# Macaron trunk on one core: four direct pairs of feed-forward tiles instead of six, the quads' input forms made product by product, and a ring of four weight units in the hybrid mixer

## The chip, the cores and the metric

The kernel runs on one core of a Trainium2 chip. The metric is the device time of one execution, in microseconds. Before the change it was run three times: the median is 1932.62 us, the lowest 1932.16, the highest 1934.15.

## What is computed

Two layers over 512 tokens of width 1024, in float32. Each layer is a feed-forward, a token mixer and a second feed-forward; the mixer of layer 0 is the hybrid one (retention and dilated attention side by side), that of layer 1 is stick-breaking attention. So there are four feed-forwards, each of hidden width 2816:

```python
def swiglu_ffn(x, g, w_in, w_out):
    h = rms_norm(x, g)
    gate, up = jnp.split(h @ w_in, 2, axis=-1)
    return (jax.nn.silu(gate) * up) @ w_out

for layer in range(DEPTH):
    x = x + 0.5 * swiglu_ffn(x, ffn1_norm[layer], ...)
    x = x + (retention_dilated_mixer if layer % 2 == 0 else stick_breaking_mixer)(x, ...)
    x = x + 0.5 * swiglu_ffn(x, ffn2_norm[layer], ...)
return rms_norm(x, final_norm)
```

## The kernel before, in words

**Three products for one.** Activations lie transposed, 128 features by 512 tokens a tile. Each float32 operand is split into a high and a low part of type float32r, and a product is made of three matmuls: high by high, high by low, low by high (`mm3`). A weight tile is 128x1024 (512 KB). It is loaded by SyncE's DMA queue into a raw slot (role `wraw`), and its parts stand in two slots of role `whl`. Two ways lead there. `weight` has ScalarE cast the high part (L224) and VectorE subtract it from the raw tile (L225). `weight_dma`, used for the hybrid mixer's input projections, has ScalarE cast the high part (L195), then make minus the high part in the slot of the low one (L196), and then a DMA from GpSimd's queue adds the weight again from DRAM (L197), so that VectorE has no part in it.

**A feed-forward** (`ffn_seven`) has 22 hidden tiles, each with a gate and an up tile. The first `DIRECT` = 6 pairs are projected directly: 24 matmuls of 512 columns for gate, as many for up. Before the first pair comes the norm's mean over the features (TensorE, role `po`), from which ScalarE and VectorE make `rr`. The other 16 hidden tiles are made by 8 quads (`quad`). A quad takes the four quarter tiles of two hidden tiles (a11, a12, a21, a22) and makes seven products (`product`: 24 matmuls of 256 columns each) in the manner of Winograd's form of Strassen's method: T3, T1, T4, B11, T2, B22, B21 by the name of the form of the input that each takes. The forms are sums and differences of quarters of the normed input, made once per feed-forward from `x` and `rr` by `normed_forms`, all before the first quad (L431 to L440, then split into high and low parts at L224 and L225). The sums of a quad's own weights are made by VectorE (p3 at L479, p1 at L485, p2 at L491, p4 at L495) and split (`cut_form`); the weights that need no sum go through ScalarE and GpSimd's queue (`cut_raw`, L450 to L452), but in the first quad of a feed-forward (`early`) a22 and a11 are split by VectorE.

**The output of a feed-forward** (`out_ffn`) has 8 tiles of 66 matmuls, whose weights come in three pieces by `weight`. Beside it runs work ahead of time for the mixers, two or so units a tile: `cut_ahead` splits a weight of the stick-breaking mixer and stores both parts to DRAM, `centre` takes the mean off a value weight of the retention heads and stores it. There are 40 such units: 16 beside the first output, 12 beside the second and 12 beside the third.

**The hybrid mixer** projects four gate tiles (`hyb_g`), then q and k of head pair 0 (`hyb_rq`, `hyb_rk`), then values of a group of heads (`values`: two weight tiles, 16 steps of six matmuls of 256 columns), and so on. A stream of projection steps is interleaved with attention: `flow.run(26)`, then the scores of head 0 (`begin(0)`), then `flow.run(27)`. After a q or k projection VectorE rotates the tile, ScalarE and VectorE split it, and `pack_q` or `pack_k` moves its halves by SyncE's queue (L654) into the layout that the scores take. 

**What sets the order.** All big tiles share 43 slots of SBUF, which roles use in turn: four slots `wraw` and six `whl` (three weight units) in the direct pairs, outputs and mixers; seven and ten in the quads. An instruction that writes a slot waits until all that read it before are done. TensorE's order is that of the program wherever `order["on"]` is set; on the other engines a scheduler puts instructions in order by their place in the program, moved ahead by `high_priority(offset)`. Every engine and every issuing queue works through its list strictly in order.

## Time and profile before

| | us |
|---|---|
| median of three runs | 1932.62 |
| the profiled execution | 1934.09 |
| span of its trace | 1932.4 |
| first feed-forward: direct pairs, quads, output | 8 to 74, 74 to 236, 236 to 357 |
| hybrid mixer | 357 to 621 |
| second feed-forward | 621 to 970 |
| third feed-forward | 970 to 1317 |
| stick-breaking mixer | 1317 to 1572 |
| fourth feed-forward and final norm | 1572 to 1932 |

The borders are read from the chain of work that ended last, rounded to whole microseconds. The trace is of one execution. "PE" is TensorE's matmuls, "PEld" its weight loads, "DVE" VectorE, "ACT" ScalarE, "POOL" GpSimd, "SPq" SyncE's sequencer issuing DMAs. Tiles are named by role. Nearly every matmul is recorded at one line (L126), so a stage is found by tiles and time, not by line. The execution's time is 1.7 us more than the span, which is what lies around it.

### The profile page before, as it was taken

The page shows a single profiled execution, that of the slowest core. Times are in us where ns is not written, and L with a number is a line of the kernel's source. Part 1 is how long each engine was busy: PE and PEld are TensorE (multiplying, and loading weights), DVE is VectorE, ACT ScalarE, POOL GpSimd, SP SyncE. Part 2 cuts the span into 40 slices and gives each one's busy share as a digit, 9 for nine tenths or more (in the row PEclk, how much of TensorE's full clock was granted, in tenths as well). Part 3 has the DMA queues.
Part 4 walks back from the last instruction along what each step waited for, and adds up shares of the span by engine and source line. Part 5 has one row for each costly group of instructions (what it writes and reads, how often), then busy time and mean ns, then how long its engine had stood idle before and what let it go on. Part 6 is the DMA issues. An engine that isn't in the chain of part 4 may idle for free.

```text
span 1932.4 us, 29858 instructions
## 1 busy us (share of the span) xinstructions
PE 1910.3 (99%) x11648; PEld 1716.8 (89%) x11648; DVE 1304.9 (68%) x1854; ACT 1059.0 (55%) x1506; POOL 165.8 (9%) x285
## 2 busy tenths in 40 slices
PE   9999999989999999999999999999999999999998
PEld 7999988778888899998889999888888888999887
DVE  8767855346777877674477677443888878777534
ACT  6466734545776456663344567332666644666423
POOL 0011000112100001100000110000222200111000
PEclk9999999999999999999999999999999999999999
DMA  6386689889852457767734775667555443767433
GB/s 228 101 202 167 140 277 338 249 225 237 178 131 84 140 140 180 167 192 254 276 131 110 197 170 148 208 225 232 161 185 152 137 137 104 201 164 163 117 92 121
DMA packets 107837, 341.00 MB, mean 176 GB/s; under 512 B 13232, under 2 KB 14896, under 8 KB 107696
## 3 DMA queue, kind: packets, MB, share of 16 engines
q1 hardware_dynamic: 90992, 278.54, 44.0%
q0 software_dynamic: 16560, 60.30, 18.0%
q8 instruction: 91, 1.49, 0.3%
q14 instruction: 50, 0.41, 0.1%
q10 hardware_dynamic: 144, 0.26, 0.0%
HBM read 280.33 MB, written 37.75 MB: 165 GB/s over the span
## 4 chain that ended last, share of the span: by engine, by line
PE 94%; DMA 3%; DVE 2%; issue 1%; ACT 1%; SPq 0%; POOL 0%; DVEq 0%; ACTq 0%; POOLq 0%
PE acc L126 46%; PE att L126 45%; PE po L126 2%; DVE whl L225 1%; DMA whl<-centred 1%; PE att L129 0%; DMA cut_sb_k<-whl 0%; DMA qk<-ah 0%; DMA qk<-sp 0%; DVE h L256 0%; DMA cut_sb_v<-whl 0%; DMA wraw<-f_out 0%; ACT whl L224 0%; DMA x<-xT 0%; DMA cut_sb_q<-whl 0%
## 5 line engine op out<-in xcount | busy, mean ns | idle before, releaser
L224 ACT CAST whl<-wraw 128x1024 fp32r<-128x1024 f32 (+4 forms) x308 | 302.8, 989 | 459.0 <-PE acc L126 199.9
L225 DVE TENSOR_TENSOR whl<-wraw,whl 128x1024 fp32r<-128x1024 f32 (+4 forms) x308 | 352.2, 1147 | 259.2 <-ACT whl L224 232.2
L126 PE MATMUL acc<-u,whl 128*128 128x512 f32 (+1 forms) x2244 | 483.5, 377 | 2.1 <-DVE whl L225 2.1
L126 PEld LDWEIGHTS acc<-u,whl 128*128 128x128 f32 x2244 | 403.3, 188 | 80.8 <-DVE whl L225 3.7
L126 PE MATMUL att<-fT,whl 128*128 128x256 f32 x3072 | 379.1, 283 | 0.0
L126 PEld LDWEIGHTS att<-fT,whl 128*128 128x128 f32 x3072 | 373.5, 192 | 0.3
L126 PE MATMUL acc<-h,whl 128*128 128x512 f32 x1248 | 302.1, 394 | 0.9 <-DVE whl L225 0.6
L126 PE MATMUL att<-fB,whl 128*128 128x256 f32 x2304 | 287.2, 283 | 0.0
L126 PEld LDWEIGHTS att<-fB,whl 128*128 128x128 f32 x2304 | 281.2, 192 | 0.2 <-DMA whl<-wq 0.2
L126 PEld LDWEIGHTS acc<-h,whl 128*128 128x128 f32 x1248 | 232.8, 188 | 53.1 <-issue 2.9
L452 POOL DMA_DIRECT2D whl<-wq x88 | 76.4, 868 | 1022.4 <-ACT whl L451 763.0
L450 ACT CAST whl<-wraw 128x1024 fp32r<-128x1024 f32 x88 | 92.4, 1050 | 83.8 <-PE att L126 83.8
L126 PE MATMUL att<-h,whl 128*128 128x512 f32 x576 | 135.8, 389 | 0.0
L126 PEld LDWEIGHTS att<-h,whl 128*128 128x128 f32 x576 | 108.4, 188 | 22.6
L451 ACT ACTIVATE whl<-whl 128x1024 fp32r<-128x1024 f32 x88 | 93.3, 1060 | 2.7
L225 DVE TENSOR_TENSOR whl<-p,whl 128x1024 fp32r<-128x1024 f32 x32 | 39.2, 1224 | 69.5 <-ACT whl L224 69.5
L126 PE MATMUL acc<-whl,h 128*128 128x256 f32 x576 | 75.9, 287 | 4.3 <-DMA whl<-centred 4.3
L126 PEld LDWEIGHTS acc<-whl,h 128*128 128x128 f32 x576 | 73.4, 194 | 5.8 <-DMA whl<-centred 4.7
L323 DVE SCALAR_TENSOR_TENSOR x<-acc,x 128x512 f32<-128x512 f32 (+1 forms) x34 | 22.4, 658 | 69.5 <-PE acc L126 69.4
L225 DVE TENSOR_TENSOR u<-uq,u 128x512 fp32r<-128x512 f32 x88 | 58.9, 688 | 13.4 <-ACT u L224 12.8
L936 POOL TENSOR_SCALAR_AFFINE_SELECT t<-t 128x128 f32<-128x128 f32 x128 | 46.2, 383 | 190.0 <-DVE t L953 124.4
L224 ACT CAST u<-uq 128x512 fp32r<-128x512 f32 x88 | 52.6, 617 | 17.3 <-PE att L126 10.3
(184 smaller groups left out, 2171.8 us busy)
## 6 DMA issues: line engine op xcount, KB each, us to landing
wraw<-wq SPq DMA_DIRECT2D x128, 512.0 KB, 5.0
whl<-wq POOLq DMA_DIRECT2D x88, 512.0 KB, 6.9
wraw<-f_out SPq DMA_DIRECT2D x68, 448.0 KB, 4.3
wraw<-wd SPq DMA_DIRECT2D x46, 512.0 KB, 3.7
wraw<-f_out SPq DMA_DIRECT2D x34, 512.0 KB, 4.7
cut_sb_q<-whl SPq DMA_DIRECT2D x16, 512.0 KB, 3.8
cut_sb_k<-whl SPq DMA_DIRECT2D x16, 512.0 KB, 3.5
cut_sb_v<-whl SPq DMA_DIRECT2D x16, 512.0 KB, 4.8
```

The costliest lines, as they stand in the source:

```text
L126: return ordered(nc.tensor.matmul(*args, **kw))
L224: nc.scalar.copy(out=hi, in_=src)
L225: nc.vector.tensor_tensor(out=lo, in0=src, in1=f32(hi), op=ALU.subtract)
L323: nc.vector.scalar_tensor_tensor(out=x[d][:, sl], in0=ps[:, sl], scalar=0.5, in1=x[d][:, sl], op0=ALU.mult, op1=ALU.add)
L450: nc.scalar.copy(out=hi, in_=raw)
L451: nc.scalar.mul(out=lo, in_=f32(hi), mul=-1.0)
L452: nc.gpsimd.dma_start(lo, src, accum_op=ALU.add)
L936: nc.gpsimd.affine_select(out=t[:, at:at + P], in_=t[:, at:at + P], pattern=[[1, P]], compare_op=ALU.is_gt, fill=0.0, base=0, channel_mult ...
```

## The change

1. `DIRECT` is 4: each feed-forward projects four pairs directly and makes nine quads instead of eight. Of the four pairs, the weights of the last two go through `weight_dma`.
2. `normed_forms` becomes a generator. It makes the eight normed tiles at once, but each form (difference and split) only as the product that takes it comes up in the program. The first quad has a22 cut by `cut_raw` ahead of its first product; a11 alone is still split by VectorE there.
3. `weight_dma` makes minus the high part straight from the raw tile (`minus_hi`) and lets the DMA go; the high part comes after it in the program.
4. In the hybrid mixer two of the four raw slots become `whl` slots: eight of them, four weight units. The scores of head 0 come after 32 steps of the stream instead of 26 (21 instead of 27 follow), and the gates are finished after three gate projections instead of two.
5. Work ahead of time: 12, 14 and 14 units beside the three outputs, and the four `centre` units come fifth to eighth instead of first.
6. Priorities: the first weight pieces of an output tile 0 and the sums of the norm are moved ahead; in the later feed-forwards the norm's mean stands one step (three matmuls) ahead of the end of the first up projection.
7. The slots of the quads' rings are the same in number (seven, ten and one), taken from other tiles.

```diff
-DIRECT = 6
+DIRECT = 4
...
+    def minus_hi(lo, src, raw):
+
+        nc.scalar.mul(out=lo, in_=raw, mul=-1.0)
+        nc.gpsimd.dma_start(lo, src, accum_op=ALU.add)
+
     def weight_dma(src, cols):
...
         nc.sync.dma_start(raw[:, :cols], src)
+        minus_hi(lo, src, raw[:, :cols])
         nc.scalar.copy(out=hi, in_=raw[:, :cols])
-        nc.scalar.mul(out=lo, in_=f32(hi), mul=-1.0)
-        nc.gpsimd.dma_start(lo, src, accum_op=ALU.add)
         return hi, lo
...
-        while pending:
-            norm_sum(*pending.pop(0))
+        with tc.high_priority(offset=2 * FIRST):
+            while pending:
+                norm_sum(*pending.pop(0))
...
-            w = weight(src[:, p0 * P:(p0 + m) * P], m * P)
+            with tc.high_priority(offset=soon):
+                w = weight(src[:, p0 * P:(p0 + m) * P], m * P)
...
-    def normed_forms(rr, gcol, work):
+    def normed_forms(rr, gcol, work, sums):
+
+        give(tf=work, tt=sums)
+        hn = []
...
+        def form(n, src):
+            fm[n] = []
+            for t in src:
+                o = B((P, 2, 2, HT), F32R, "f" + n)
+                split(o[:, 0], o[:, 1], t)
+                fm[n].append(o)
+
+        def less(a, b, sign=1.0):
+
+            t = B((P, 2, 2, HT), F32, "tt")
+            for kk in range(2):
+                nc.vector.scalar_tensor_tensor(out=t[:, kk], in0=a[kk], scalar=sign, in1=b[kk],
+                                               op0=ALU.mult, op1=ALU.subtract)
+            return [t[:, kk] for kk in range(2)]
+
+        t3 = less(b22, b12)
+        form("T3", t3)
+        yield fm
+        form("T1", less(b11, b12))
+        yield fm
+        t2 = less(t3, b11, -1.0)
+        form("T4", less(t2, b21, -1.0))
+        yield fm
...
+        form("B21", b21)
...
     def quad(wq, fm, uq, early):
...
+        if early:
+            w22 = cut_raw(a22, wq[3])
...
-        product(bc, cut_form(p3), fm["T3"], True)
+        product(bc, cut_form(p3), next(fm)["T3"], True)
...
-                w2 = [weight(wd[i], D) for i in (f, DIRECT + f)]
+                w2 = [(weight if f < 2 else weight_dma)(wd[i], D) for i in (f, DIRECT + f)]
...
-                proj_tile(None, pu, w2[1])
-                rr = rms()
-                act_set(SILU)
+                for k, _ in enumerate(proj_steps(None, pu, w2[1])):
+                    if k == 6:
+                        rr = rms()
+                        act_set(SILU)
...
-        give(wraw=oldest("wraw") + ext[:3], p3=ext[3:], whl=oldest("whl") + old[4:])
+        ring = oldest("whl")
+        give(wraw=ext[:1] + oldest("wraw") + old[6:], p3=ext[1:2], whl=ring[:4] + ext[2:] + ring[4:] + old[4:6])
...
     def hybrid(ss, gcol_next):
...
         mixer_roles()
+        raws, ring = oldest("wraw"), oldest("whl")
+        give(wraw=raws[2:], whl=ring + raws[:2])
...
-        flow.run(26)
+        flow.run(32)
...
         begin(0)
-        flow.run(27)
+        flow.run(21)
...
-    ahead = [lambda k=("hyb_rv", g, u): centre(k) for g in range(2) for u in range(2)]
-    ahead += [lambda u=u: cut_ahead(*u) for u in sb]
+    ahead = [lambda u=u: cut_ahead(*u) for u in sb]
+    ahead[4:4] = [lambda k=("hyb_rv", g, u): centre(k) for g in range(2) for u in range(2)]
...
-    ss = out_ffn(a["f1_out"][0], us, 8, ahead, 16)
+    ss = out_ffn(a["f1_out"][0], us, 8, ahead, 12)
```

Where the order moves, on three engines. First TensorE in the hybrid mixer, before: `acc_568` is the second half of the values of the first heads, and the `att` rows are the first scores of head 0, which read the packed q and k (`qk`, `qlo`).

```order
L126 MATMUL acc_568_3811<-whl_563_3746,h_399_2804 128x256
L126 MATMUL acc_568_3811<-whl_562_3745,h_399_2804 128x256
L126 MATMUL att_569_3824<-qk_550_3688,qk_559_3738 128x384
L126 MATMUL att_569_3824<-qlo_505_3458,qk_559_3738 128x384
L126 MATMUL att_569_3824<-qk_550_3688,qk_559_3738 128x128
L126 MATMUL att_569_3824<-qlo_505_3458,qk_559_3738 128x128
L126 MATMUL att_571_3834<-qk_550_3688,qk_559_3738 128x256
L126 MATMUL att_571_3834<-qlo_505_3458,qk_559_3738 128x256
L126 MATMUL att_573_3841<-qk_550_3688,qk_559_3738 128x512
L126 MATMUL att_573_3841<-qlo_505_3458,qk_559_3738 128x512
L126 MATMUL acc_568_3811<-whl_562_3745,h_417_2914 128x256
```

And the same place after the change, where `acc_562` is that second half and `acc_571` the next q projection.

```order
L126 MATMUL acc_562_3874<-whl_560_3840,h_498_3518 128x256
L126 MATMUL acc_562_3874<-whl_559_3839,h_498_3518 128x256
L126 MATMUL att_563_3923<-qk_544_3751,qk_553_3801 128x384
L126 MATMUL att_563_3923<-qlo_499_3521,qk_553_3801 128x384
L126 MATMUL att_563_3923<-qk_544_3751,qk_553_3801 128x128
L126 MATMUL att_563_3923<-qlo_499_3521,qk_553_3801 128x128
L126 MATMUL att_565_3933<-qk_544_3751,qk_553_3801 128x256
L126 MATMUL att_565_3933<-qlo_499_3521,qk_553_3801 128x256
L126 MATMUL att_567_3940<-qk_544_3751,qk_553_3801 128x512
L126 MATMUL att_567_3940<-qlo_499_3521,qk_553_3801 128x512
L126 MATMUL acc_571_3954<-h_389_2794,whl_573_3956 128x512 x2
```

The scores stood after two of the eight steps of that half, and now stand behind all eight: six steps of six matmuls have moved ahead of them.

Second, ScalarE in the second feed-forward at the norm, before: `whl_1033` is the high part of the gate weight of the third pair, the `t` rows are the logarithm and exponential of the norm.

```order
L224 CAST whl_1033_6271<-wraw_1032_6270 128x1024
L108 ACTIVATE t_1012_6182<-po_1011_6180,eps_n_72 128x512
L108 ACTIVATE t_1013_6184<-t_1012_6182 128x512
L102 ACT_TABLE_LOAD
L108 ACTIVATE t_1017_6194<-tp_1016_6192 128x512
```

After the change the same weight is `whl_1027` (high) and `whl_1028` (minus high, on which GpSimd's DMA waits); `t_1006` and `t_1007` are the norm's.

```order
L108 ACTIVATE t_1006_6242<-po_1005_6240,eps_n_72 128x512
L201 CAST whl_1027_6334<-wraw_1026_6333 128x1024
L108 ACTIVATE t_1007_6244<-t_1006_6242 128x512
L102 ACT_TABLE_LOAD
L193 ACTIVATE whl_1028_6335<-wraw_1026_6333 128x1024
L108 ACTIVATE t_1011_6257<-tp_1010_6255 128x512
L201 CAST whl_1030_6341<-wraw_1029_6340 128x1024
```

The scheduler has put the high part first here all the same, and the minus stands behind the norm's two functions and a table load.

Third, VectorE in the second feed-forward around the first quad, before: `whl_1110` is the low part of that quad's first weight (p3), and the last two pairs' products (L553, L560) stand around it.

```order
L553 TENSOR_TENSOR tp_1061_6445<-acc_1054_6408,r_1015_6189 128x512
L225 TENSOR_TENSOR whl_1072_6487<-wraw_1070_6485,whl_1071_6486 128x1024
L560 TENSOR_TENSOR tp_1064_6474<-att_1063_6449,r_1015_6189 128x512
L563 TENSOR_TENSOR uq_1065_6476<-tp_1064_6474,t_1062_6447 128x512
L225 TENSOR_TENSOR whl_1110_6629<-p3_1104_6622,whl_1109_6628 128x1024
L479 TENSOR_TENSOR p3_1133_6853<-wraw_1130_6846,wraw_1129_6845 128x1024
```

After the change the same weight is `whl_1061`; `tp_1044` is the gate of the fourth and last direct pair, `fT4`, `fB11` and `fT2` are low parts of forms.

```order
L229 TENSOR_TENSOR fB11_1082_6628<-tf_1062_6499,fB11_1082_6628 128x512
L229 TENSOR_TENSOR fT4_1078_6593<-tt_1077_6590,fT4_1078_6593 128x512
L584 TENSOR_TENSOR tp_1044_6443<-acc_1037_6404,r_1009_6249 128x512
L229 TENSOR_TENSOR fT4_1079_6596<-tt_1077_6590,fT4_1079_6596 128x512
L229 TENSOR_TENSOR whl_1061_6496<-p3_1053_6484,whl_1060_6495 128x1024
L229 TENSOR_TENSOR fB11_1083_6631<-tf_1063_6500,fB11_1083_6631 128x512
L229 TENSOR_TENSOR fT2_1087_6664<-tt_1076_6587,fT2_1087_6664 128x512
L229 TENSOR_TENSOR fT2_1088_6667<-tt_1076_6587,fT2_1088_6667 128x512
L229 TENSOR_TENSOR whl_1086_6661<-wraw_1051_6478,whl_1085_6660 128x1024
```

Before, every form was done when the first quad's weights were split; now some forms of the later products stand behind them, among the first quad's own work.

72 lines of the change are left out of this document (35 added, 37 removed).

## The prediction

> **What bounds the kernel now.** First the page: how busy each engine is, and the chain of work that ended last.
>
> ```profile
> PE 1910.3 (99%) x11648; PEld 1716.8 (89%) x11648; DVE 1304.9 (68%) x1854; ACT 1059.0 (55%) x1506; POOL 165.8 (9%) x285
> PE 94%; DMA 3%; DVE 2%; issue 1%; ACT 1%; SPq 0%; POOL 0%; DVEq 0%; ACTq 0%; POOLq 0%
> ```
>
> TensorE is the bound almost everywhere. So a change pays in two ways only: less time of matmuls, or fewer waits of TensorE. For the first, the chain in order of time gives rates, here in the second feed-forward (start, us, what):
>
> ```profile
> 627.02 5.44 PE att L126 x24
> 632.46 0.86 PE po L126 x2
> 633.32 5.48 PE acc L126 x24
> ...
> 682.32 166.77 PE att L126 x1368
> ```
>
> A direct projection is 24 matmuls of 512 columns in 5.44 us, 226.7 ns each. The last row holds the last up projection (24, so 5.44 us) and eight quads of 168 matmuls of 256 columns: (166.77 - 5.44) / 1344 = 120.0 ns each, with no wait among them. For the second way, the waits of TensorE, over the whole span (us in total, times, longest), then in the stretch of the first output and in that of the second:
>
> ```profile
> PE acc L126 <- DMA whl<-centred: 4.3, 2, 3.2
> PE att L126 <- DMA qk<-ah: 3.0, 1, 3.0
> PE acc L126 <- DVE whl L225: 2.7, 3, 1.5
> ...
> PE acc L126 <- DVE whl L225: 1.5, 1, 1.5
> PE acc L126 <- DVE whl L225: 0.7, 1, 0.7
> ```
>
> All that the change could win here is 4.3 + 3.0 in the hybrid mixer, 1.5 at the first output's end, and 0.7 and 0.6 (the rest of 2.7) at two seams.
>
> **1. One quad for two direct pairs.** Per feed-forward it removes 4 x 24 matmuls at 226.7 ns, 21.76 us, and adds 168 at 120.0 ns, 20.16 us: 1.6 us less, 6.4 us in four. Both prices hold where weights come in time; items 2 and 3 ask whether they do.
>
> **2. The weights of pairs three and four come by GpSimd's DMA.** They cost VectorE nothing any more, but have a longer way. These rows are ScalarE at the norm of the second feed-forward, from the timeline, then the landings of GpSimd's accumulating DMAs in the quads and in the hybrid mixer:
>
> ```profile
> 633.35 0.69 ACT L108 ACTIVATE t<-po,eps_n 128x512 f32<-128x512 f32 x1
> 634.08 0.63 ACT L108 ACTIVATE t<-t 128x512 f32<-128x512 f32 x1
> 634.73 1.28 ACT L102 ACT_TABLE_LOAD   x1
> ...
> L451 ACT ACTIVATE whl<-whl 128x1024 fp32r<-128x1024 f32 x88 | 93.3, 1060 | 2.7
> L450 ACT CAST whl<-wraw 128x1024 fp32r<-128x1024 f32 x88 | 92.4, 1050 | 83.8 <-PE att L126 83.8
> ...
> DMA to landing us min/median/max: 5.3/6.9/8.8
> DMA to landing us min/median/max: 5.3/6.9/10.2
> ```
>
> The third gate weight may be cast when the first up projection frees its slot, at 633.3. In the new order ScalarE then does cast 1.05, exponential 0.63, table load 1.28, minus 1.06: 637.35. GpSimd issues about 0.36 later (item 4's rows show such a gap, 392.45 + 1.06 to 393.87), at 637.7. TensorE wants the low part with its third matmul of the third gate: 633.32 + 2 x 5.44 + 0.45 = 644.7. So the landing may take 7.0 us. At the median of 6.9 nothing is lost; at 5.3 there is time to spare; at 8.8 it is 1.8 us late, and the fourth up weight, whose slot comes free after that late gate, some 0.5 more. The other two have a margin of 1 to 2 us, since no norm stands in their way. In the first feed-forward the minus comes ahead of the exponential and the slot is free earlier. I take 0.3 us in three feed-forwards, **+1.0**, nearest to the median; ends 0 and 3 x 2.3 = +7. What is queued behind a late weight on GpSimd is only the next of these DMAs.
>
> The Trainium skill (DMA: Bandwidth & Descriptors, the section on the anatomy of one DMA on GpSimd's path) fits such a DMA as 2.0 us plus bytes over 436e3 per us, which for 512 KB makes 3.2 us. The trace's median of 6.9 us is double that; by the page's figure this term would be 0 and the sum 1.0 us lower. The trace decides.
>
> **3. The forms one product at a time, in less time.** VectorE works in order, so it is asked whether its work before and in the first quad still fits. These two windows are direct pairs two to six of the second feed-forward, and its first quad (from:to, length, busy of PE, PEld, DVE, ACT, POOL, clock, DMA share, GB/s); then four rows of VectorE's timeline right after the norm's factor rr is there, and the loads of the quads (count, KB, us to landing):
>
> ```profile
> 632.75:687.80 55.05, 55.05 (x244) 45.42 (x243) 48.08 (x64) 24.87 (x34) 0.00 (x0) 1.00 0.33 108
> 687.80:707.90 20.10, 20.10 (x169) 20.10 (x168) 15.59 (x18) 12.47 (x13) 2.18 (x3) 1.00 0.54 143
> ...
> 636.92 0.69 DVE L553 TENSOR_TENSOR tp<-acc,r 128x512 f32<-128x512 f32 x1
> ...
> 639.39 0.68 DVE L553 TENSOR_TENSOR tp<-acc,r 128x512 f32<-128x512 f32 x1
> 639.99 1.21 DVE L225 TENSOR_TENSOR whl<-wraw,whl 128x1024 fp32r<-128x1024 f32 x1
> 641.12 2.07 DVE L431 SCALAR_TENSOR_TENSOR tf<-x,gains,r 128x512 f32<-128x512 f32 x3
> ...
> wraw<-wq SPq DMA_DIRECT2D x128, 512.0 KB, 5.0
> ```
>
> The records overlap a little: from start to start an instruction of 512 elements takes 0.60 us, of 1024 1.13. VectorE was busy 63.7 of 75.2 us. The stretch becomes 75.2 - 21.8 = 53.4 us. Its work loses eight weight splits (pairs three to six) and that of a22, 9 x 1.13, and six products of the dropped pairs, 6 x 0.60: 13.8 us, which leaves 49.9, or 93%. It fits with 3.5 us to spare, if the order asks for few waits. In the new order the split of p3, with which the first quad begins, is the 38th instruction from rr: 5 x 1.13 and 33 x some 0.62, 26 us, from 636.9 to 663. In it I let VectorE wait 2 us for a11, whose raw slot comes free only with the minus of item 2 (637.35, and 5.0 to land); that makes 665. The quad starts at 633.32 + 6 x 5.44 = 666.0. What stands behind (B11, T2, B22, B21) has two to six products of 2.88 us (24 x 120.0 ns) more. So **0**, with 1 us in hand; the ends are 0 and the price of the third rival. ScalarE, busy 24.87 + 12.47 of 75.2, has room for the minus of two weights a pair.
>
> **4. The hybrid mixer.** The timeline where both its waits fall:
>
> ```profile
> 388.56 0.86 POOL L197 DMA_DIRECT2D whl<-centred  x1 [2.90 <-ACT whl L196]
> 391.39 3.15 PE L126 MATMUL acc<-whl,h 128*128 128x256 f32 x25
> 392.45 1.06 ACT L196 ACTIVATE whl<-whl 128x1024 fp32r<-128x1024 f32 x1
> 393.87 0.86 POOL L197 DMA_DIRECT2D whl<-hyb_rq  x1 [4.45 <-ACT whl L196]
> 394.28 0.63 ACT L648 ACTIVATE ah<-tp 128x512 fp32r<-128x512 f32 x1 [0.76 <-DVE tp L729]
> 395.05 0.98 SPq L734 DMA_DIRECT2D o<-rot_k  x1
> 396.14 4.14 SPq L654 DMA_DIRECT2D qk<-ah  x4
> 397.71 4.46 PE L126 MATMUL acc<-whl,h 128*128 128x256 f32 x35 [3.16 <-DMA whl<-centred]
> 405.21 0.42 PE L126 MATMUL att<-qk,qk 128*128 128x384 f32 x1 [3.05 <-DMA qk<-ah]
> ```
>
> The value weight issued at 388.56 came at 397.7, 9.1 us later, and TensorE had waited 3.16. Its slot was freed by the projection three units before it; with four units it is freed one projection, 5.44 us, earlier, which covers the wait with 2.3 to spare. The second such wait (4.3 - 3.2 = 1.1) has the same cause. Both go: **-4.3**. The raw ring falls to two slots, but a load, 5.0 us in the quads, still has one projection's 5.44 us, and in the new order of SyncE's queue the moves of k stand ahead of the table rot_k that took 0.98 at 395.05.
>
> The scores wait for k: from the end of its projection (391.39) to 405.21 pass 13.8 us. Before, ten steps of six matmuls of 120.0 ns lay between, 7.2 us, and the 3.16 of the other wait. Now sixteen lie there: 11.5 us. Without the table ahead the way is some 12.8; with a less crowded queue, less. So 1.0 of the 3.0 is left, **-2.0**; ends 0 (another DMA as slow takes its place) and -3.0.
>
> **5. Fewer units beside the first output.** These windows are the first and the second output.
>
> ```profile
> 235.64:355.00 119.36, 117.87 (x519) 96.83 (x518) 66.55 (x71) 48.81 (x56) 1.84 (x2) 1.00 0.84 294
> 849.00:968.00 119.00, 118.35 (x522) 97.44 (x522) 59.19 (x64) 47.44 (x56) 0.00 (x0) 1.00 0.74 254
> ```
>
> The first moved 294 GB/s x 119.4 us = 35 MB and had 1.5 us of wait; four units less are 4 x 1.5 MB (0.5 loaded, 1.0 stored), 6 MB less, about the second's traffic. The wait goes, **-1.5** (ends -1.5 and -0.8, the second's wait). The second and the third get two units more, 3 MB each, and come halfway to the first: **+0.4** (ends -0.7 and +0.8, the first's).
>
> **6. The rest at nothing.** The earlier mean moves three matmuls, 0.68 us, across a row that cost the same before and after; the two hidden functions of item 2 bound what follows. The priorities at the outputs' first tiles find no wait there to remove. The gates' later finish frees three `acc` banks for the fourth gate after 5.44 us of the third's projection, longer than the norm's some 4 us. The 0.6 at the second feed-forward's start stays.
>
> Sum: -6.4 + 1.0 + 0 - 4.3 - 2.0 - 1.5 + 0.4 = **-12.8 us**. From the profiled execution's 1934.09 that is 1921.3; this execution lay 1.5 above the median of 1932.62, from which I forecast **1920 us**.
>
> **The rivals.** *The hybrid mixer's waits only move*: the gain there of 6.3 is lost to the next late DMA (the queue of SyncE took 4.14 us to issue four moves): 1926. For it: the DMA engines' share in that stretch (last but one column):
>
> ```profile
> 355.00:405.00 50.00, 44.01 (x222) 36.97 (x220) 16.20 (x27) 23.69 (x28) 9.50 (x10) 1.00 0.93 227
> ```
>
> Against: the ring's extra unit is worth more than each wait.
>
> *The weights of item 2 come late*: at 8.8 us a landing the term is +7 instead of +1, 1926; at the hybrid's slowest, 10.2, each of three feed-forwards loses 3.2 + 1.9 and the first some 2, 1936, just level. It decides from 7.0 us. For it: a median almost at the limit. Against: the direct pairs kept the DMA engines busy for 0.33 of the time, so their landings should be nearer to 5.3 than to 8.8.
>
> The Trainium skill (SBUF — State Buffer, who interferes with whom) gives a reason for such lateness: an operation of VectorE in a two-port mode keeps GpSimd from writing its DMA's descriptors. It names copies and casts for that and not tensor_tensor, which VectorE mostly runs here.
>
> *VectorE becomes the bound, and the kernel slower*: in the stretch of item 3 it stood idle 75.2 - 63.7 = 11.5 us before, in waits for ScalarE's casts, loads and TensorE. It can now afford 3.5. If all 11.5 stay, the first quad starts or runs 8 us late in each feed-forward, 32 in four: 1952. It is slower by over 0.2% from (12.8 + 3.9) / 4 = 4.2 us a feed-forward, when 7.7 of the 11.5 stay. For it: p3's split stands behind forms that only the third and fourth products take. Against: most of the old waits were of one kind, here from the waits of that stretch (us in total, times, longest):
>
> ```profile
> DVE whl L225 <- ACT whl L224: 8.7, 7, 2.6
> ```
>
> Those were splits of weights whose cast waited for a slot that TensorE still read; of such weights few are left.
>
> **How the numbers follow.** 0.2%, 3.9 us, is about what a measurement of this kernel can tell from no change. My case 0.72; the mixer's waits move 0.12; late weights 0.09, in a third of it level; VectorE the bound 0.07, most of it slower. Faster 0.88, same 0.06, slower 0.06. The range takes the best ends, -6.4 - 7.3 - 1.5 - 0.7 = -15.9 and 0.6 more at the seam, 1916, with 1 us for the scatter; above it reaches past the first rival and the milder form of the second to 1929.
>
> **What would show it.** Right: the chain has pieces of 24 + 9 x 168 = 1536 matmuls in about 186.9 us; the waits on whl<-centred are gone and that on qk<-ah is about 1 us; none on whl L229 at the first output's end. Wrong: TensorE waiting for `whl` from `wd` (item 2), or for whl or fT at the first quad (item 3); matmuls of 256 columns slower than 120.0 ns; a hybrid mixer whose stretch is not about 6 us shorter.

## The result, and the profile after

The changed kernel takes 1938.4 us (median; 1935.2 to 1941.2), the kernel before 1932.0 on the same chip: a ratio of 1.0029 with a 95% interval of 1.0019 to 1.0039. A second comparison gave 1.0046 (1.0032 to 1.0060). So the change costs 6 to 9 us, where the prediction had nearly 13 us of gain. The profiled execution of the first comparison took 1935.8 us, span 1934.1, the low end of its runs; a second profile of the same kernel has a span of 1940.7. Both are used. One execution of the run u_hyb below took 3799 us for no reason that its record shows, and its ratio leaves that one out.

The page's first row, and the chain of work that ended last, of the changed kernel:

```profile
PE 1908.1 (99%) x11936; PEld 1724.9 (89%) x11936; DVE 1299.5 (67%) x1854; ACT 1100.2 (57%) x1558; POOL 193.7 (10%) x317
PE 84%; DMA 6%; issue 5%; DVE 3%; ACT 1%; POOL 0%; SPq 0%; DVEq 0%; POOLq 0%; ACTq 0%
```

The busy shares hardly differ from before; the chain does. TensorE carried 94% of it before and carries 84% now, and DMA has gone from 3% to 6%. The quads themselves are as forecast, as the chain in order of time shows in the second feed-forward (start, us, what):

```profile
660.88 186.87 PE att L126 x1536
```

This piece is the 24 + 9 x 168 = 1536 matmuls in 186.9 us that were to show the first term right. What went wrong is in the waits of TensorE over the whole span (us in total, times, longest), in the first profile and in the second:

```profile
PE att L126 <- DMA wraw<-hyb_dq: 4.5, 1, 4.5
PE acc L126 <- DMA whl<-wd: 3.0, 3, 1.1
PE acc L126 <- DVE whl L229: 2.4, 6, 0.6
PE att L126 <- DMA qk<-ah: 2.3, 1, 2.3
```

```profile
PE att L126 <- ACT t L812: 4.8, 1, 4.8
...
PE acc L126 <- DMA whl<-wd: 3.2, 3, 1.2
PE att L126 <- DMA whl<-wd: 1.7, 1, 1.7
PE att L126 <- DMA qk<-ah: 1.6, 1, 1.6
```

The waits on whl<-centred are gone, as forecast, but a single one of 4.5 to 4.8 us has come, at 441 and 444 us. It is one and the same matmul of the retention norm; the first profile puts its wait down to a DMA that had only just gone out, the second to ScalarE's square (L812), which is the input. On qk<-ah 2.3 and 1.6 us are left of 3.0, where about 1 was forecast. New too are the waits on weights of pairs three and four (`wd`), and small ones on VectorE's splits in the second output (1.8 us there in the first profile, 0.7 before).

Each stage's length, read from its last matmul and that of the stage before, gives the account (us, after minus before; the direct pairs of the fourth feed-forward are counted with the stick-breaking mixer ahead of them; two direct pairs, 21.76, are taken off the direct stages of before, and a quad, 20.16, is counted with the quads):

| stage | forecast | first profile | second profile |
|---|---|---|---|
| quads, four feed-forwards, without the dropped pairs | -6.4 | -6.4 | -6.3 |
| direct pairs of the first, third and fourth feed-forward | +0.7 | +3.2 | +5.3 |
| hybrid mixer and the direct pairs behind it | -6.0 | +3.9 | +5.5 |
| first output | -1.5 | -2.2 | -2.2 |
| second and third output | +0.4 | +2.7 | +5.6 |
| sum | -12.8 | +1.2 | +7.9 |

The spans differ by 1.7 and 8.3, so a few tenths lie outside these stages. Ten of the fourteen us that the first profile lacks are in one row, the hybrid mixer's.

This is the place, in the changed kernel's timeline (SP is SyncE's queue issuing DMAs):

```profile
423.85 1.05 ACT L193 ACTIVATE whl<-wraw 128x1024 fp32r<-128x1024 f32 x1
...
432.54 0.55 SPq L686 DMA_DIRECT2D qlo<-sp  x1
434.66 0.33 SPq L199 DMA_DIRECT2D wraw<-hyb_rk  x1
...
441.43 1.06 ACT L193 ACTIVATE whl<-wraw 128x1024 fp32r<-128x1024 f32 x1 [4.00 <-DMA wraw<-hyb_rk]
...
443.44 0.58 ACT L731 COPY t<-po 64x512 f32<-64x512 f32 x1
444.78 0.63 ACT L812 ACTIVATE t<-oo 128x512 f32<-128x512 f32 x1 [0.76 <-DVE oo L732]
...
445.46 2.07 PE L126 MATMUL att<-t,bd 128*128 128x512 f32 x2 [4.53 <-DMA wraw<-hyb_dq]
```

ScalarE's last read of a raw slot ends at 423.85 + 1.05 = 424.9, so both are free; yet the load of the next k weight goes out at 434.66, behind q's moves in SyncE's queue, and ScalarE begins on it 6.8 us later. ScalarE, in order, stands for 4 us at minus that weight, and behind it stands the norm that TensorE needs.

The wait is not all of the loss. Windows at its end and behind it (from:to, length, busy of PE, PEld, DVE, ACT, POOL, granted clock, DMA share, GB/s):

```profile
443.90:450.70 6.80, 5.24 (x15) 4.02 (x16) 3.48 (x7) 4.98 (x10) 1.59 (x3) 0.50 0.98 213
450.70:455.00 4.30, 4.30 (x33) 4.08 (x32) 3.69 (x6) 2.92 (x5) 1.30 (x4) 1.00 0.90 216
```

The granted clock is 0.50 up to 450.7 and 1.00 from there. TensorE works through 5.24 us of that stretch at half speed, which is 2.6 us more, behind a wait of 4.5. The prediction had no term for this. The Trainium skill (TensorE: Matmul & The Clock Gate, Part 1, the HAM clock gate) has a clock of half speed after an idle window of about 3.4 us, in windows that run freely; the trace agrees with the half. It does not agree that a whole window has to be idle: a wait of 3.04 us was enough in ring3 below.

### The profile page after: what moved, and what is told of

Read it like the earlier page. It is cut to its first block, busy times and chain, and to the rows that moved or that the text cites. A ratio compares the mean times of both kernels' runs of the same rounds, so it can differ in the third digit from the quotient of the medians.

```text
span 1934.1 us, 30592 instructions
## 1 busy us (share of the span) xinstructions
PE 1908.1 (99%) x11936; PEld 1724.9 (89%) x11936; DVE 1299.5 (67%) x1854; ACT 1100.2 (57%) x1558; POOL 193.7 (10%) x317
## 4 chain that ended last, share of the span: by engine, by line
PE 84%; DMA 6%; issue 5%; DVE 3%; ACT 1%; POOL 0%; SPq 0%; DVEq 0%; POOLq 0%; ACTq 0%
PE att L126 43%; PE acc L126 39%; PE po L126 2%; DMA wraw<-hyb_rq 1%; DMA whl<-wd 1%; DVE whl L229 1%; DMA cut_sb_k<-whl 1%; DMA o<-rot_k 1%; DVE h L260 1%; DMA whl<-wq 0%; PE att L129 0%; DMA qk<-ah 0%; ACT whl L193 0%; DMA cut_sb_v<-whl 0%; DMA wraw<-sb_q 0%
## 5 line engine op out<-in xcount | busy, mean ns | idle before, releaser
L126 PE MATMUL att<-fT,whl 128*128 128x256 f32 x3456 | 426.4, 283 | 0.0
L126 PEld LDWEIGHTS att<-fT,whl 128*128 128x128 f32 x3456 | 420.1, 192 | 0.3
L126 PE MATMUL att<-fB,whl 128*128 128x256 f32 x2592 | 323.0, 283 | 0.0
L126 PEld LDWEIGHTS att<-fB,whl 128*128 128x128 f32 x2592 | 316.3, 192 | 0.2 <-DMA whl<-wq 0.2
L126 PE MATMUL acc<-h,whl 128*128 128x512 f32 x1056 | 257.4, 394 | 4.2 <-DMA whl<-wd 3.0
L126 PEld LDWEIGHTS acc<-h,whl 128*128 128x128 f32 x1056 | 196.4, 188 | 49.9 <-DMA whl<-wd 4.6
L479 ACT CAST whl<-wraw 128x1024 fp32r<-128x1024 f32 x104 | 109.1, 1049 | 110.1 <-PE att L126 108.9
L126 PE MATMUL att<-h,whl 128*128 128x512 f32 x384 | 93.0, 393 | 0.0
L126 PEld LDWEIGHTS att<-h,whl 128*128 128x128 f32 x384 | 72.3, 189 | 16.7 <-issue 1.4
L201 ACT CAST whl<-wraw 128x1024 fp32r<-128x1024 f32 x43 | 44.9, 1047 | 32.6 <-PE acc L126 16.5
L108 ACT ACTIVATE t<-t 128x512 f32<-128x512 f32 (+1 forms) x100 | 57.2, 590 | 5.1 <-DVE t L537 2.8
```

The lines of the kernel that those rows point to most:

```text
L108: r = nc.scalar.activation(out=o, in_=i, func=f, **kw)
L126: return ordered(nc.tensor.matmul(*args, **kw))
L201: nc.scalar.copy(out=hi, in_=raw[:, :cols])
L479: nc.scalar.copy(out=hi, in_=raw)
```

## The experiments

All were compared with the kernel before on the same chip. "Waits" are TensorE's in the profiled execution of each run: in the hybrid mixer from 355 to 460 us, and for weights of pairs three and four, each summed over the trace's rows. The profiled execution is one of the run's several, so its waits need not be those of the median.

| run | median, us | ratio (95%) | mixer's waits | waits on wd |
|---|---|---|---|---|
| kernel before | 1932.0 | 1 | 7.3 | 0 |
| changed kernel, first | 1938.4 | 1.0029 (1.0019 to 1.0039) | 7.9 | 3.0 |
| after_2: the same again | 1941.4 | 1.0046 (1.0032 to 1.0060) | 9.5 | 4.9 |
| u_hyb | 1934.2 | 1.0009 (0.9999 to 1.0018) | 6.4 | 3.2 |
| u_wd | 1932.0 | 0.9994 (0.9985 to 1.0003) | 8.9 | 0 |
| u_units | 1936.7 | 1.0014 (1.0005 to 1.0023) | 6.3 | 3.5 |
| u_all | 1929.3 | 0.9978 (0.9968 to 0.9988) | 4.9 | 0 |
| ring3 | 1932.5 | 0.9997 (0.9988 to 1.0006) | 4.2 | 5.1 |
| minus3 | 1936.8 | 1.0014 (1.0006 to 1.0023) | 6.6 | 1.9 |
| bquads | 1958.3 | 1.0130 (1.0117 to 1.0144) | 6.4 | 0 |
| poolload | 1941.8 | 1.0044 (1.0032 to 1.0057) | 9.1 | 5.2 |
| ring37 | 1935.1 | 1.0013 (1.0002 to 1.0023) | 3.2, and 3.0 at 461 | 5.0 |
| ring3_wd | 1925.2 | 0.9961 (0.9947 to 0.9975) | 4.9 | 0 |
| ring3_wd_units | 1924.2 | 0.9956 (0.9943 to 0.9968) | 2.1 | 0 |
| after_vsplit | 1925.7 | 0.9964 (0.9952 to 0.9977) | 1.4 | 4.1 |
| ring4_vsplit | 1921.1 | 0.9937 (0.9924 to 0.9949) | 0.5 | 0 |
| ring3_vsplit | 1921.2 | 0.9938 (0.9924 to 0.9951) | 0 | 0 |
| before_vsplit | 1924.0 | 0.9957 (0.9943 to 0.9971) | 0.2 | 0 |
| ring4_vsplit_14 | 1920.9 | 0.9949 (0.9936 to 0.9961) | 0 | 0 |

### One part undone at a time

u_hyb takes back the hybrid mixer's part of the change: ring, steps and gates.

```diff
-        raws, ring = oldest("wraw"), oldest("whl")
-        give(wraw=raws[2:], whl=ring + raws[:2])
...
-            if p < 2:
                 continue
-            if p == 2:
+            if p == 1:
...
-        flow.run(32)
+        flow.run(26)
...
-        flow.run(21)
+        flow.run(27)
...
```

> The changed kernel with the hybrid mixer's ring, steps and gates as before (three units, 26 and 27 steps, gates after two). Theory A (the ring's two raw slots are a new wait: the casts of a late weight stand in ScalarE's list ahead of what the retention norm needs, 4.5 us at 441): the 4.5 us wait of the norm's matmul goes, the waits on whl<-centred (4.3) and qk<-ah (3.0) come back; against the changed kernel's 1938.4 it is 1 to 4 us faster, and scatters less. Theory B (the mixer's change is worth what was forecast, and the loss lies in the feed-forwards): it is 6 us slower, about 1944.

It measured 1.0009, 3.9 us below the changed kernel. The mixer's part costs time, then, and is not the whole loss. With the old ring the old waits are back (3.0 on whl<-centred, 3.6 on qk<-ah).

u_wd has VectorE split the weights of pairs three and four:

```diff
-                w2 = [(weight if f < 2 else weight_dma)(wd[i], D) for i in (f, DIRECT + f)]
+                w2 = [weight(wd[i], D) for i in (f, DIRECT + f)]
```

> The changed kernel with the weights of the third and fourth pairs split by VectorE again. Theory A (each of three feed-forwards waits 1.1 to 1.4 us for GpSimd's DMA at the third gate weight, 3.8 in all, more in slower executions): those waits go and nothing takes their place, 4 us faster than the changed kernel, about 1934. Theory C (VectorE has no room: four splits of 1.13 us, 4.5, against 3.5 spare): the first quad waits instead, 1 to 3 us a feed-forward, and it is level with the changed kernel or up to 8 us slower.

It measured 0.9994, 6.8 us below the changed kernel, and the waits on `wd` are gone. The rest of the gain is not explained by them. VectorE, which now has these splits again, is nearly full in its windows of the second feed-forward, up to the first quad and in it, but TensorE stands still in neither:

```profile
627.50:657.50 30.00, 30.00 (x132) 24.48 (x131) 26.22 (x37) 14.04 (x18) 0.00 (x0) 1.00 0.36 118
657.50:677.50 20.00, 20.00 (x136) 18.58 (x135) 19.83 (x29) 12.75 (x19) 1.74 (x2) 1.00 0.61 160
```

PE is busy for all of both (second number), DVE for 26.22 of 30 and 19.83 of 20. So the DMA way for these weights relieves an engine that had just enough time, and costs TensorE waits.

u_units has 16, 12 and 12 units, `centre` first; u_all undoes all three, and leaves the quads, their forms and the priorities:

```diff
-    ss = out_ffn(a["f1_out"][0], us, 8, ahead, 12)
+    ss = out_ffn(a["f1_out"][0], us, 8, ahead, 16)
...
-    ss = out_ffn(a["f2_out"][0], us, 24, ahead, 14)
+    ss = out_ffn(a["f2_out"][0], us, 24, ahead, 12)
...
```

> The changed kernel with 16, 12 and 12 units ahead of time, the centred ones first, as before. Theory A (14 units beside the second output cost 2.6 us there, the four fewer beside the first gain 1.9): within 1 us of the changed kernel; the waits of the second output fall from 2.4 to about 0.7, that of 1.5 at the first output's end comes back. Theory D (the fewer units beside the first output are what relieves the mixer's start): 3 us or more slower, with longer waits for hyb weights.

> The changed kernel with all three undone: what is left is four direct pairs, forms product by product, minus ahead of hi in the mixer's weights, priorities. If the quads' 6.4 us are real in the time and VectorE has room, 1932.0 - 6.4 = 1925.6. If VectorE has no room (theory C), 1929 to 1934. If the loss is in something else that is left (a matmul rate, the forms), 1932 or more.

u_units measured 1.0014; its first output is 1.9 us longer than the changed kernel's, so the four units less do win what was forecast there. The second output did not get shorter with twelve units (124.9 us, 123.6 in the changed kernel's first profile), so the first theory is wrong there. Where the run's 2.9 us against the changed kernel come from is not shown: the profiled execution was its slowest (1938.8 us). Its waits in the mixer are other ones (6.3) without an edit there, a first sign that they do not belong to one edit. u_all measured 0.9978: with the rest undone, 4.3 us of the quads' 6.4 are on the clock. That is in the range of the theory that VectorE has no room, but TensorE waits for VectorE in none of its quads.

### The ring, the third weight, and the forms

after_2 is the changed kernel again, as the base of this call:

> The changed kernel once more, unchanged, as the base for the runs beside it and for a second profile of it. If the reading of its first profile holds, the same waits of TensorE stand in it again: some 4.5 us at 441 behind the load of a hyb_rk weight, some 1 us for the third gate weight in each of three feed-forwards (3 to 4 in all), 2 to 3 on qk<-ah; the time is again 1.002 to 1.004 of the kernel before, 1936.5 to 1940. If those waits were chance, they are elsewhere in this profile and the time may be anywhere from 1931 to 1941.

The long wait, those on `wd` and that on qk<-ah stood in it again; at 1.0046 its time was a little above what was expected.

ring3 takes back the ring alone:

```diff
-        raws, ring = oldest("wraw"), oldest("whl")
-        give(wraw=raws[2:], whl=ring + raws[:2])
...
-        raws, ring = oldest("wraw"), oldest("whl")
-        give(wraw=raws + ring[:2], whl=ring[2:])
```

> The changed kernel with only the hybrid mixer's ring as before (four raw slots, six of role whl); 32 steps of the stream before the first scores and the later gates stay. Theory ring: two raw slots let a load go out only behind the moves of q in SyncE's queue, so the wait of 4.5 us at 441 goes, the waits on whl<-centred come back with 2 to 4, qk<-ah stays at 1 to 4, and the time is 2 to 4 us below the changed kernel. Rival: the 32 steps or the later gates cause that wait, so it stays and the time is within 1 us of the changed kernel's or, with whl<-centred back, 2 to 4 us above it.

0.9997, 9 us below after_2 and 6 below the first comparison: more than either theory had. (In the profiles 5.9 us of the difference to after_2 are in the mixer's row and 3.3 in the second output, which the edit does not touch.) The 4.5 us wait is gone, that on qk<-ah is down to 0.2 (3.0 before), and whl<-centred is back with 4.2. The 32 steps did what they were to do; with the DMA engines as full as they are here, the ring is what cost. With four raw slots the load that was late goes out ahead of q's moves, from the timeline of SyncE's queue in ring3:

```profile
415.97 0.33 SPq L199 DMA_DIRECT2D wraw<-hyb_rk  x1
417.45 1.20 SPq L686 DMA_DIRECT2D qk<-sp  x2
```

minus3 exchanges the two slots of the third gate weight, so that minus the high part stands ahead of the exponential and the table load on ScalarE:

```diff
...
+        if first:
+            hi, lo = lo, hi
...
-                w2 = [(weight if f < 2 else weight_dma)(wd[i], D) for i in (f, DIRECT + f)]
+                w2 = [weight(wd[i], D) if f < 2 else weight_dma(wd[i], D, i == 2) for i in (f, DIRECT + f)]
```

> The changed kernel with one edit: for the third gate weight of a feed-forward the slots of the two parts are exchanged, so that ScalarE makes minus the high part before the exponential and the table load of the norm, and the high part after them. Theory start: the DMA of the third gate weight is late because it is let go 2 to 3 us later than it could be; it is issued some 3 us earlier in feed-forwards two to four, the three waits of TensorE on whl<-wd (3.0 in all) fall below 0.5, and the time is 2 to 4 us below the changed kernel. Rival landing: the DMA takes 8 us and more whenever it is issued, or the next three weights are late as well: 2 us or more of waits on whl<-wd stay and the time is within 1 us of the changed kernel. Third: the high part is late in its stead (a wait on ACT whl of 1 us or more).

1.0014, 6 us below after_2, of which 3.0 are the waits on `wd` (4.9 to 1.9). The rows that tell it, of the changed kernel and of minus3, in the second feed-forward:

```profile
633.87 1.28 ACT L102 ACT_TABLE_LOAD   x1
635.16 1.06 ACT L193 ACTIVATE whl<-wraw 128x1024 fp32r<-128x1024 f32 x1
...
636.59 0.86 POOL L194 DMA_DIRECT2D whl<-wd  x1 [101.70 <-ACT whl L193]
...
644.71 5.28 PE L126 MATMUL acc<-h,whl 128*128 128x512 f32 x22 [1.06 <-DMA whl<-wd]
```

```profile
634.94 0.86 POOL L194 DMA_DIRECT2D whl<-wd  x1 [98.54 <-ACT whl L193]
...
644.28 5.60 PE L126 MATMUL acc<-h,whl 128*128 128x512 f32 x24
```

Issued at 636.59 the DMA is there at 644.67, 8.1 us later, and TensorE has stood for 1.06. In minus3 this feed-forward runs 1.2 us later, the issue comes 1.65 earlier all the same, and the 24 matmuls run without a gap. Its landing was shorter too, 5.4 us, but 8.1 from that start would also have been in time. So an earlier start is enough here. Of the 1.9 us left 1.4 are in the first feed-forward, where ScalarE's order was this one already and the landing alone is late.

bquads is the kernel before with `DIRECT` at 4 and nothing else, all forms ahead of the first quad:

> The kernel before with one edit: four direct pairs and nine quads instead of six and eight; the weights of pairs three and four still by VectorE, all forms still made before the first quad. If VectorE has the time (theory: the order of the forms is not needed), the quads' gain shows alone: 1926 to 1928, 6 us below the kernel before. If the order is needed (my working of VectorE, as in the prediction): the split of p3 stands 48 instructions behind rr instead of 38, some 32 us, so the first quad starts 3 to 11 us late in each feed-forward, TensorE waits there for fT3 or whl of VectorE, and the time is 1938 to 1965.

1.0130: 25 us slower than before, where the quads alone would make it 6 faster, so some 8 us a feed-forward are lost. The waits in its four first quads, over the span:

```profile
PE att L126 <- ACT whl L224: 9.9, 4, 4.2
PE att L126 <- DVE whl L225: 5.4, 4, 1.5
```

With the second of these waits and a lowered clock behind them (0.50 for 3.4 or 6.8 us), nine quads take 184.9 to 186.1 us from their first matmul, where the changed kernel takes 181.6 to 181.9. The third rival of the prediction, 8 us late in each feed-forward, is what happens without the forms made product by product.

### Is it the queue, the ring, or the DMA engines?

poolload issues the mixer's raw loads from GpSimd's queue, past the moves of q; ring37 gives one raw slot to the ring instead of two:

```diff
-        nc.sync.dma_start(raw[:, :cols], src)
+        (nc.gpsimd if order["hyb"] else nc.sync).dma_start(raw[:, :cols], src)
...
```

```diff
-        give(wraw=raws[2:], whl=ring + raws[:2])
+        give(wraw=raws[1:], whl=ring + raws[:1])
...
```

> The changed kernel (ring of four units kept) with one edit: in the hybrid mixer the raw loads of weights are issued from GpSimd's queue instead of SyncE's, so that they do not stand behind the moves of q and k. The changed kernel stood at 1.003 and 1.0046 of the kernel before in two comparisons. Theory queue: a load late because it is queued in order behind moves, not because two raw slots are too few; the wait of 4.5 us at 441 to 449 falls below 0.5, no wait on whl<-centred comes back, and the time is 0.998 to 1.001 of the kernel before. Rival slots: two raw slots are too few wherever the load is issued, so a wait of 3 us or more stays in that stretch and the ratio is 1.002 or more. It can also be worse than both if a load from GpSimd's queue takes much longer than SyncE's 5 us, or holds up the DMAs that add the weights.

> The changed kernel with a middle dose of item 4: one raw slot goes over to role whl instead of two (three raw, seven whl). Theory queue: with three raw slots the load of hyb_rk finds its slot free ahead of the moves of q, so the wait of 4.5 us goes as with four, and half a unit more of whl takes a part of the 4.2 us on whl<-centred; 0.998 to 1.000 of the kernel before, at or 1 to 3 us below the run with four raw slots (0.9997). Rival: each raw slot less costs in proportion, so half the loss stays: 1.002.

poolload gained nothing (1.0044). The wait at 441 is gone, but two others stand in its timeline, both for k's moves, though the first is put down to "issue" (one of the moves landed at 408.40):

```profile
408.49 0.62 PE L126 MATMUL att<-qk,qk 128*128 128x384 f32 x1 [4.79 <-issue]
...
439.53 0.69 PE L126 MATMUL att<-qk,qk 128*128 128x384 f32 x1 [2.88 <-DMA qk<-ah]
```

It isn't a clean test of the queue, since a load took 9.2 us (the median of the hyb_rq loads) by this way. ring37 lies between the others (1.0013): 2.9 us on whl<-centred up to 460, and a new wait of 3.0 for a hyb_rk weight at 461. With each of these arrangements something is late, and always behind a DMA. That is what full DMA engines would do. Here is the stretch from 355 to 450 of the kernel before, then of the changed one (queues: packets, MB, share of the 16 engines' time; issues: count, KB, median us to landing):

```profile
q1 hardware_dynamic: 5212, 14.27, 48.1%
q0 software_dynamic: 2016, 7.34, 43.0%
...
wraw<-hyb_rq SPq DMA_DIRECT2D x3, 512.0 KB, 4.1
wraw<-hyb_rk SPq DMA_DIRECT2D x3, 512.0 KB, 5.1
```

```profile
q1 hardware_dynamic: 5549, 15.37, 50.4%
q0 software_dynamic: 2176, 7.93, 44.7%
...
wraw<-hyb_rq SPq DMA_DIRECT2D x4, 512.0 KB, 8.0
wraw<-hyb_rk SPq DMA_DIRECT2D x4, 512.0 KB, 9.0
...
qk<-ah SPq DMA_DIRECT2D x12, 128.0 KB, 7.0
```

The DMA engines are busy for 91% before and 95% after, and the adding DMAs (q0) take nearly half of it for a third of the bytes. But the share of the whole stretch does not set a load's time: the loads of hyb_rq and hyb_rk take 4.1 and 5.1 us before and 8.0 and 9.0 after, and in ring3, at a share of 0.94, 5.6 and 5.1. What differs is when they run: four of these loads of the kernel before lie between 370.2 and 392.1, where the share is 0.80, and four of ring3 meet 0.85; three of the changed kernel lie between 377.3 and 394.2, where it is 1.00. The moves of k take 7.0 to 8.0 in all three. So the test is to take their traffic away, at either ring. after_vsplit has VectorE make the low parts of the mixer's first weights:

```diff
-    BY_DMA = ["hyb_" + n for n in ("g", "rq", "rk", "rv", "dq", "dk", "dv")]
+    BY_DMA = ["hyb_" + n for n in ("dq", "dk", "dv")]
```

ring4_vsplit adds to it u_wd's edit and 12, 12, 16 units; ring3_vsplit is ring4_vsplit with the ring of before. The two runs with that ring and without the edit of `BY_DMA`, ring3_wd and ring3_wd_units, had come first.

> The changed kernel with the hybrid mixer's ring as before and the weights of direct pairs three and four split by VectorE, as before; the 32 steps, the later gates, nine quads with their forms one at a time and the units 12, 14, 14 stay. If the two losses are apart from each other, the 4.8 us of waits on whl<-wd come off the run with the ring alone (0.9997): 0.997 to 0.998 of the kernel before, 1927 to 1928. If VectorE is then late at the first quad or its splits are late, waits on whl of VectorE take their place and it stays at 0.999 to 1.000.

> The run beside it with one more edit: 12, 12 and 16 units beside the three outputs instead of 12, 14 and 14. The second output has then the units it had before and should lose its 2 to 3 us of waits on VectorE's splits; the third has the sixteen that the first had before, which cost 1.5 to 2.2 there. If the loss is due to the number of units, 0 to 2 us below the run beside it. If the second output loses its time for another reason, the same or up to 2 us above it.

> The changed kernel (ring of four units, two raw slots) with one edit: in the hybrid mixer the low parts of the weights of gates, retention q, k and values are made by VectorE from the raw tile instead of by DMAs that add the weight again; dilated q, k and values stay with the DMA. Theory traffic: the DMA engines are the bound from 355 to 450 (0.89 to 1.06 of their time), so with half of the weight traffic gone the waits there (6.8 to 7.6 us and the lower clock behind the long one) fall below 2, and the ratio is 0.998 to 1.000 where the changed kernel has 1.003 to 1.0046. Rival ring: two raw slots are too few for whatever traffic, so a wait of 3 us or more stays and the ratio is 1.002 or more. Third: VectorE (0.33 to 0.45 busy there) is late with the rotations in its stead: waits on whl of VectorE or qk<-ah above 3 us.

> The run beside it (ring of four, VectorE splits in the first half of the mixer) with the weights of direct pairs three and four by VectorE too and units 12, 12, 16. With the ring of before, these two edits took the ratio from 0.9997 to 0.9956, 8 us. Theory traffic: with the DMA engines no bound, the ring of four does no harm: 0.992 to 0.996, within 2 us of the run with the ring of before and the same splits. Rival ring: 3 us or more above that run.

> The run ring3_wd_units (0.9956: ring of before, weights of pairs three and four by VectorE, units 12, 12, 16) with the weights of gates, retention q, k and values split by VectorE. Theory traffic: its last 2.1 us of waits on whl<-centred go, 0.994 to 0.995, some 2 us below it. If VectorE's queue is the next bound, its splits stand behind the rotations: waits on whl of VectorE of 2 us or more there and 0.996 to 0.999. If the ring were the bound and not the traffic, nothing changes: 0.9956.

The two losses add up: ring3_wd measured 0.9961, 1.7 us below what was expected, less than its interval can tell. Between it and ring3_wd_units (0.9956) nothing can be told. But their traces show how far chance goes in that stretch: the code of the mixer is the same, and it took 5.9 us less in the second. The same 71 matmuls in ring3_wd_units, and in ring3:

```profile
394.20 8.78 PE L126 MATMUL acc<-whl,h 128*128 128x256 f32 x71 [1.75 <-DMA whl<-centred]
```

```profile
396.05 11.29 PE L126 MATMUL acc<-whl,h 128*128 128x256 f32 x71 [3.04 <-DMA whl<-centred]
```

The wait of 3.04 cost 11.29 - 8.78 = 2.5 us of lower clock on top of itself; that of 1.75 cost none.

after_vsplit measured 0.9964, better than expected: one line, and the changed kernel is 13 us faster than in its first comparison; in the profiles 10.5 us of that are in the mixer's row. The same view of it from 355 to 450, its window, and that of before_vsplit:

```profile
q1 hardware_dynamic: 5825, 16.39, 57.4%
q0 software_dynamic: 168, 0.62, 4.2%
...
wraw<-hyb_rq SPq DMA_DIRECT2D x4, 512.0 KB, 4.9
wraw<-hyb_rk SPq DMA_DIRECT2D x4, 512.0 KB, 4.3
...
qk<-ah SPq DMA_DIRECT2D x12, 128.0 KB, 2.3
```

```profile
355.00:450.00 95.00, 93.59 (x518) 81.46 (x517) 59.34 (x92) 42.05 (x61) 10.77 (x20) 1.00 0.62 180
```

```profile
355.00:450.00 95.00, 94.77 (x524) 82.45 (x522) 59.80 (x94) 40.32 (x59) 10.30 (x19) 1.00 0.62 173
```

The DMA share is 0.62, a load with two raw slots takes 4.3 to 4.9 us again, k's moves 2.3, and one wait of 1.4 is left. VectorE took the work (59 of 95 us busy, 37 before) and TensorE does not wait for it there. ring4_vsplit and ring3_vsplit are level, 0.9937 and 0.9938: with room on the DMA engines the ring makes no difference. Both beat the two kernels of the case, by 11 to 12 us the one before. So the loss takes both: the ring of four costs 6 to 9 us beside full DMA engines (ring3) and nothing measurable beside engines with room. The theory that two raw slots are too few for whatever traffic falls.

One rival is not separated. The edit takes away traffic, and with it the adding DMA and ScalarE's pass out of each weight's own way, so that nothing is left for a wait on whl<-centred to wait for. That traffic counts shows in transfers that the edit does not touch: k's moves fall from 7.0 to 2.3 us, the raw loads from 8 and 9 to 4.9 and 4.3. How much of the gain is due to each, no run here shows.

Two runs more ask what the change is worth with this out of the way, and what the units cost. before_vsplit gives the kernel before the same line; ring4_vsplit_14 is ring4_vsplit with 12, 14 and 14 units:

> The kernel before with one edit: in the hybrid mixer the low parts of the weights of gates, retention q, k and values are made by VectorE instead of by adding DMAs. Theory traffic: its own 7.3 us of waits between 355 and 450 and some 1.5 us of lowered clock behind them come from the same full DMA engines and go: 0.995 to 0.996. Set against after_vsplit (0.9964), the change without the mixer's waits is then worth what the rest of its terms measured, -6.4 + 4.5 - 2.2 + 2.7 = -1.4 us, within 0.001 of level. Rival: the waits of the kernel before are those of its ring and steps, not of traffic: 3 us or more of them stay and the ratio is 0.998 or more.

> The run ring4_vsplit (0.9937) with the units of the change, 12, 14 and 14, instead of 12, 12 and 16; all else the same. If the number of units sets the loss beside an output, the third output loses its 4 us and the second, which took 3.2 us beyond the least with twelve, takes up to 2 us more: 0.992 to 0.993. If units cost nothing as such: 0.9937 within 0.0005 and the third output keeps its loss.

before_vsplit measured 0.9957, as expected, its mixer's waits gone too. Against after_vsplit (0.9964) the change is level: the quads' 6.4 us and the first output's 2.2 are spent by the late `wd` weights, the second output and the last 1.4 us of wait in the mixer. ring4_vsplit_14 (0.9949 against 0.9937, medians 1920.9 and 1921.1) shows no difference in time that holds, and lies outside both expectations. In its profile the third output is 4.1 us shorter (119.7 instead of 123.8), so sixteen units do cost there; the second took 124.7 us with fourteen units and 124.0 with twelve. Over all profiles of kernels with the change's quads the second output took 121.9 to 126.6 us with fourteen (eleven profiles, mean 124.4) and 121.4 to 124.9 with twelve (five, mean 122.7): the number may carry a part, but does not decide alone.

## Why the prediction was wrong

**Item 1** held to the tenth: 120.0 ns a matmul, 1536 in 186.87 us, -6.4 us.

**Item 2** was mis-sized. The time left for the landing was right: the DMA was let go at 636.59 and wanted at 643.65, 7.1 us later, where the prediction had 7.0. The landing was taken at the 6.9 us of the quads; these sixteen DMAs have a median of 8.0 (the last number):

```profile
whl<-wd POOLq DMA_DIRECT2D x16, 512.0 KB, 8.0
```

and the argument that direct pairs leave the DMA engines idle, so landings should be nearer to 5.3, failed. Its 0.33 was a mean over 55 us of the kernel before. In the changed kernel loads for the quads run in the same time, and the DMA share (last but one) around this one DMA is:

```profile
636.60:640.00 3.40, 3.40 (x17) 2.82 (x16) 3.27 (x6) 3.06 (x4) 0.91 (x2) 1.00 0.66 166
640.00:644.70 4.70, 3.65 (x17) 2.68 (x15) 4.60 (x7) 2.63 (x5) 0.80 (x1) 1.00 0.94 214
```

Whether VectorE held GpSimd up as well, the prediction's second reason for lateness, no run here tests. (The 3.2 us that the prediction took from the Trainium skill, DMA: Bandwidth & Descriptors, the anatomy of one DMA on GpSimd's path, is further off still.) It cost about 4.5 us (3.2 in three feed-forwards and 1.3 in the second) where +1.0 stood, inside the ends of 0 and +7; u_wd, whose time has other effects in it, puts it at 6.8.

**Item 3** held: TensorE waits for no form and no split at a quad. Making all forms ahead of the quad does not work (bquads); the relief of VectorE by DMAs was not needed for it (u_wd).

**Item 4** is where the forecast failed: -6.3 stood there, and the mixer took 2.6 us more in the first profile (3.9 less 1.3 of item 2). The step that failed is that two raw slots are enough, so that the ring's gain of 4.3 costs nothing. It rested on "a load, 5.0 us in the quads, still has one projection's 5.44 us". The ring did take the waits on whl<-centred away, 4.3 to 0. But in the mixer of the changed kernel a load takes 8 to 9 us, and the one that mattered went out 9.8 us after its slot was free, behind q's moves; the prediction looked at k's moves in that queue, and not at what q's wait for. In place of 4.3 us came a wait of 4.5 and 2.6 of lowered clock behind it, for which there was no term.

The second half, the steps, was right as a mechanism: 3.0 us on qk<-ah became 0.2 in ring3. In the changed kernel itself 2.3 and 1.6 are left where 1.0 was forecast.

Behind the failed step stands another: that a slot more takes away a wait for a DMA when the profile shows the DMA engines busy for 0.93 of the stretch. That row stood in the prediction, as support for the first rival, and was set aside because the unit "is worth more than each wait". Here the ring decided which transfers came late. At shares of 0.94 and 0.95, ring3 has loads of 5 to 6 us and 4.2 on whl<-centred, the changed kernel loads of 8 to 9, nothing on whl<-centred and the long wait. The first rival, the waits only move, is what happened, at a higher price than it was given: it set the term at 0.

**Item 5** was right for the first output (-2.2; forecast -1.5) and the third (0), and missed the second, +2.7 and +5.6 where +0.2 stood. There the chain of the second profile goes from store to load to split and back:

```profile
929.23 7.63 DMA cut_sb_k<-whl
...
940.50 5.66 DMA wraw<-sb_v
...
947.40 5.99 DMA cut_sb_k<-whl
...
955.12 5.24 DMA wraw<-f_out
```

A store frees the slot that the next split waits for, so in this stretch a round of these transfers, not TensorE, sets the pace. What decides whether a run has 121.4 or 126 us there stays open; the priority of item 6 and other slots of the ring were not tried by themselves.

## What to carry to other kernels

Before a change in buffers or order is credited with a wait on a DMA, look at the DMA share of that stretch: near 0.9, as here, a further slot may only choose which transfer is late, and it was less traffic that removed the waits. Take a transfer's time from the place in which it will run, not from another stretch and not from a mean; and where an engine stands at 0.4 beside full DMA engines, move the work to it, one line of which was worth more here than seven items. Count a long wait with the lowered clock behind it. Parts that each pay only if the others do should be run one by one.

## What the runs showed of the hardware

- An adding DMA of GpSimd's queue occupies the DMA engines longer for its bytes: by the packets' times 7.93 MB took 44.7% of their time where 15.37 MB of plain DMAs took 50.4%, 1.7 times as long per byte; in the kernel before the factor is the same.
- A transfer's time to landing follows the crowd: moves of 128 KB took 7.0 us at a DMA share of 0.95 and 2.3 at 0.62. The crowd is that of the moment: with a share of 0.94 to 0.95 over the stretch, loads of 512 KB took 5 to 6 us in ring3 and 8 to 9 in the changed kernel.
- In the 14 of 19 traces that have a lowered clock amid the work it is 0.50, for 3.4 or 6.8 us, which made a wait of 3.0 us cost 5.5 and one of 4.5 cost 7.1. The wait's length alone does not decide. Cut each trace, but for its start and its end, into pieces of 3.41 us in line with its lowered stretches: every piece at full clock in which TensorE was idle for 1.89 us or more was followed by a lowered one, none with 1.67 or less was, and in between it went both ways. So in the kernel before a wait of 3.16 us, 1.4 of it in one piece and 1.7 in the next, cost no clock, and one of 3.05, with 2.4 in one piece, did.
